# The reciprocal root of x moved from the query projection into the key projection, in a layer whose order is fixed by a planner

## The chip, the cores and the metric

The kernel runs on one core of a Trainium2 chip. The metric is the time of one execution on the device in microseconds (us). The core's engines are TensorE (PE; its weight loads are shown apart as PEld), VectorE (DVE), ScalarE (ACT), GpSimd (POOL) and SyncE (SP, which here issues the large transfers). Each engine works off its own instructions in order, and they wait for one another through semaphores.

## The reference, cut to what matters

```python
# x: (1, 256, 2048); 16 meta tokens are put ahead, so h has 272 rows
u = rms_norm(h, norm_mix)                 # h * rsqrt(mean(h*h) + 1e-6) * gain
proj = einsum('bld,dc->blc', u, w_in)     # 2048 -> aq, ak, av (1024 each), mq, mk, mv, mo, mg
aq, ak, av, mq, mk, mv, mo, mg = split(proj)
attn_out = diff_attention(rope(aq), rope(ak), av, ...)   # 8 heads, two softmaxes each
ml_out = mlstm_mixer(mq, mk, mv, mo, mg, ...)            # mg: the gates, 16 columns
h = h + concat(attn_out, ml_out) @ w_out
u = rms_norm(h, norm_ffn)
h = h + (silu(u @ w_gate) * (u @ w_up)) @ w_down         # 2048 -> 5632 -> 2048
return rms_norm(h, norm_final)[:, 16:]
```

The factor `rsqrt(mean(h*h))` is one number for each token. The kernel does not scale x by it ahead of the projections: it multiplies the unscaled x by the weights (with the gain put into the weights), and puts the factor in behind them. For queries and keys it goes into the rotary tables (`ropeC`, `ropeS`), which multiply them anyway; for the gates it is a multiplication by `rbc`, a tile that holds the factor of each token on every partition.

## The kernel before, in words

Every product is made in three parts for accuracy. A weight w is split into a high part `wh` and the rest `wl` (lines 205 and 206: ACT makes `wh` with the gain `gm`, DVE makes `wl` from `raw`, `gm` and `wh`), the activation into `uh` and `ul`, and PE adds `wh`·`uh`, `wh`·`ul` and `wl`·`uh` (lines 251, 252 and 253). Weights come in pieces of 256 rows by 512 columns (512 KB, loaded by SP into `raw_...`), each split in two halves of 128x512. There are four buffers of each of `raw`, `wh` and `wl`. A projection of 512 columns has 8 pieces and four accumulators; per piece there are 24 matmuls.

The stages follow one another on PE: the first half of the query projection (`aq_0` to `aq_7`, line 426, together with the transposes of x and their splits `uhl`, lines 405 and 406), then of the key projection (`ak`) and of the value projection (`av`), then the second halves of the three, the projections of the second mixer, the output projection, and the feed-forward part.

The order on each engine is made by a planner: it simulates the program with costs of its own and puts an instruction where it expects it to be ready. `pin(instruction)` keeps an instruction in program order. In a projection a `slot()` is called at every second piece; it takes the next step of the generators in the list `urgent`, so that small work comes between the matmuls of the large one.

The parts that the change touches:

- `x_rstd` (lines 344 to 355) makes the reciprocal root of the three token groups in 14 small steps on DVE and writes it out wide as `rmat` (line 355). It is run, pinned, among the last weight splits of the query projection (`rstd_steps`). `x_broadcast` (lines 357 to 365) turns it into a row on every partition with three matmuls into `prs` (a small PSUM tile, of which there are two) and copies that to `rbc` on ACT (line 365). Then DVE and POOL multiply the rotary tables by it (lines 489 and 490).
- `setup` transposes small vectors and makes the factor lambda (`lexp`, `nlam`, line 509).
- `gates` makes the gates of the second mixer: POOL multiplies the gate weights `wg` by the gain (line 564), ACT casts them to `wgp` (line 565), PE makes `pgate`, DVE multiplies it by `rbc` to `gsb` (line 574), PE makes `psi` (line 585), and a chain of small steps follows: `gi_ga` and `gfr` on DVE (lines 586 to 589), abs, exp and log on ACT (590 to 592), then on DVE `gi_ga` (594), two running sums (596, 597), a subtraction (600), two running maxima (603, 604) and more. The end of it, `pct`, is a set of transposes on PE.
- `rope` rotates a head pair: a shuffle and a multiplication on DVE (lines 840 and 841), a multiplication and an addition on POOL (842 and 843). `value_copy` takes an accumulator out of PSUM into `vt_...` on ACT (line 631).
- `in_proj(..., pins=n)` pins the splits of the first n pieces; before, the first key projection has 4 and the value projection none.

Of the kernel before, what the change touches and what calls it, by code (L numbers as in the profile page):

```python
# [86 lines left out]
def tile_hybrid_encoder_layer(  # L87
# [36 lines left out]
    def sm_tile(name):  # L124
        return smp.tile([P, N_CHUNK], F32, tag="sm", name=name)
# [4 lines left out]
    def f(ap):  # L130
        return ap.bitcast(F32)
# [66 lines left out]
    def pin(ins):  # L198
        tc.keep_in_program_order(ins)
# [86 lines left out]
    rmat = ep.tile([P, 3, P], F32, name="rmat")  # L286
# [48 lines left out]
    def x_square(i):  # L335
# [4 lines left out]
                accum_out=ssx[:, 4 * b + c:4 * b + c + 1],  # L340
            )
        )

    def x_rstd():
        ms, y, t, h = (rs3[:, 3 * i:3 * i + 3] for i in range(4))
        yield V.tensor_reduce(ms[:, 0:2], ssx[:, :8].rearrange("p (b c) -> p b c", c=4), AX.X, ALU.add)
        yield V.tensor_copy(ms[:, 2:3], ssx[:, 8:9])
        yield V.tensor_scalar(ms, ms, 1.0 / D, EPS, ALU.mult, ALU.add)
        yield V.tensor_scalar(y.bitcast(I32), ms.bitcast(I32), -0.5, RSQRT_MAGIC, ALU.mult, ALU.add)
        yield V.tensor_scalar(h, ms, -0.5, None, ALU.mult)  # L350
        for _ in range(3):
            yield V.tensor_tensor(t, y, y, ALU.mult)
            yield V.tensor_tensor(t, t, h, ALU.mult)
            yield V.scalar_tensor_tensor(y, t, 1.5, y, ALU.add, ALU.mult)
        yield V.tensor_copy(rmat, rs3[:, 3:6, None].to_broadcast([P, 3, P]))

    def x_broadcast():
        prs = sm_tile("prs")
        pin(T.matmul(prs[:, :NM], lhsT=rmat[:NM, 2, :], rhs=ident[:NM, :NM], start=True, stop=True))
        for b in range(NB):  # L360
            pin(T.matmul(
                prs[:, NM + b * P:NM + (b + 1) * P], lhsT=rmat[:, b, :], rhs=ident,
                start=True, stop=True,
            ))
# [67 lines left out]
    rstd = x_rstd()

    def rstd_steps(n):
        for _ in range(n):
            ins = next(rstd, None)
            if ins is not None:
                pin(ins)
# [121 lines left out]
    colt = mp.tile([P, 5, 64], F32, name="colt")  # L560

    def gates():
        wgp = mp.tile([P, KD, 32], F32R, tag="t2", bufs=3, name="wgp")
        G.tensor_tensor(wg, wg, gm[:, :, None].to_broadcast([P, KD, 16]), ALU.mult)
        A.copy(wgp[:, :, :16], wg)
# [267 lines left out]
    def rope(ps, t0, name, h):  # L833
        n = NT - t0
        if t0:
            qk[h] = pair_tile(f"qk{h}")
        dst = qk[h][:, 0 if t0 else 1, :n]
        sh = mp.tile([P, NT], F32, tag="ev", bufs=4, name=f"sh_{name}")
        swap = list(range(8, 16)) + list(range(8)) + list(range(16, 32))
        V.stream_shuffle(sh[:, :n], ps[:, :n], swap)  # L840
        V.tensor_tensor(dst, ps[:, :n], ropeC[:, t0:], ALU.mult)
        G.tensor_tensor(sh[:, :n], sh[:, :n], ropeS[:, t0:], ALU.mult)
        G.tensor_tensor(dst, dst, sh[:, :n], ALU.add)
        return dst
# [7 lines left out]
    def attention(h0, nh):  # L852
        es, at, hs, on, qs, ks = {}, {}, {}, {}, {}, {}

        def stack(h):
            q, k = aq[h], ak[h]
            qs[h] = mp.tile([P, 2, SEQ], F32R, tag="qs", bufs=2, name=f"qs{h}")
            ks[h] = mp.tile([P, 2, 2, HT], F32R, tag="ks", bufs=2, name=f"ks{h}")
            kz = klow[h % 2]
            for c in range(2):  # L860
                own, other = slice(64 * c, 64 * c + 64), slice(64 - 64 * c, 128 - 64 * c)
                A.activation(qs[h][own, c, :], q[own], AF.Copy, scale=QK_SCALE)
                kc = apart(k[own])
                A.copy(ks[h][own, c], kc)
                A.copy(ks[h][other, c], kc)
                V.scalar_tensor_tensor(
                    qs[h][other, c, :], q[own], QK_SCALE, f(qs[h][own, c, :]), ALU.mult, ALU.subtract
                )
                V.tensor_tensor(kz[own, c], kc, f(ks[h][own, c]), ALU.subtract)

        def stats(h):
            g = h // 2
# [81 lines left out]
                yield  # L954
        attending.remove(h0)

    def roping(vts, t0, dst, name, g):
        def hook(i):
            if 1 <= i <= 4:
                dst[4 * g + i - 1] = rope(vts[i - 1], t0, f"{name}_{4 * g + i - 1}", 4 * g + i - 1)  # L960

        return hook

    for g in range(2):
        if g:
# [15 lines left out]
        urgent.append(value_natural(vts, lambda j, g=g: val[:, :, 4 * g + j, :], f"a{g}"))  # L981
        pending.append(attention(4 * g, 4))
# [256 lines left out]
```

## Time and profile before

| | us |
|---|---|
| median of 3 runs | 1125.45 |
| the three runs | 1124.95, 1125.45, 1127.51 |
| profiled execution | 1124.79 |
| its span | 1123.0 |
| query projection, PE, first to last matmul | 5.9 to 36.6 |
| key projection begins, value projection begins | 36.6, 64.1 |
| next query projection begins | 90.4 |

The span is the time from the first to the last instruction in the profile. A row of the timeline has the start, the duration, the engine, the line, the operation, what it writes and reads, and in square brackets how long the engine was idle before it and what it waited for.

### The profile page before, as it was taken

How to read it: one execution, taken by the hardware profiler on the slowest of the kernel's cores; microseconds unless marked ns; L12 is line 12 of the kernel's file. 1: busy time of each engine (PE TensorE's matmuls, PEld its weight loads, DVE VectorE, ACT ScalarE, POOL GpSimd, SP SyncE). 2: the span in 40 equal slices, each digit the busy share in tenths (PEclk: the TensorE clock that was granted, in tenths of full speed). 3: DMA queues.
4: the chain of work that ended last, by engine and by line, in shares of the span. 5: the costliest groups of instructions: out<-in, count | busy, mean ns of one | idle time of the engine just before them, and what ended most of it. 6: DMA issues, size and time to landing. Idle time of an engine off the chain costs nothing.

```text
span 1123.0 us, 18984 instructions
## 1 busy us (share of the span) xinstructions
PE 1108.5 (99%) x7181; PEld 1025.4 (91%) x7181; DVE 737.6 (66%) x1151; ACT 659.3 (59%) x1205; POOL 243.9 (22%) x315
## 2 busy tenths in 40 slices
PE   9999999999999999999999999999999999999997
PEld 8999999999999989999999999999999888888896
DVE  6996987988785987655655655655655645454544
ACT  6578888788976555554554554554554544344443
POOL 7330240010043944122122122122122100000000
PEclk9999999999999999999999999999999999999998
DMA  9556555555445675575665665665665766666663
GB/s 276 169 149 205 147 165 159 152 151 154 148 152 160 202 235 179 192 228 184 199 220 184 200 217 188 201 213 187 205 209 187 251 205 198 205 192 204 193 204 111
DMA packets 112539, 212.78 MB, mean 189 GB/s; under 512 B 8938, under 2 KB 10288, under 8 KB 112304
## 3 DMA queue, kind: packets, MB, share of 16 engines
q1 hardware_dynamic: 111664, 209.95, 59.8%
q10 hardware_dynamic: 464, 1.58, 0.4%
q8 instruction: 56, 0.92, 0.3%
q14 instruction: 35, 0.29, 0.1%
q0 software_dynamic: 320, 0.04, 0.0%
HBM read 209.45 MB, written 2.10 MB: 188 GB/s over the span
## 4 chain that ended last, share of the span: by engine, by line
PE 92%; DVE 4%; DMA 1%; issue 1%; ACT 1%; SPq 1%; POOL 0%; DVEq 0%; ACTq 0%; POOLq 0%
PE acc_up L248 14%; PE acc_ga L248 14%; PE acc_ga L249 7%; PE acc_up L249 7%; PE acc_dn L1129 7%; PE acc_dn L1126 7%; PE acc_dn L1130 7%; PE acc_wo L248 3%; PE acc_mo L248 3%; PE acc_wo L249 2%; PE acc_mv L251 1%; PE acc_mv L253 1%; PE acc_mv L252 1%; PE acc_mo L249 1%; PE acc_av L253 1%; PE acc_av L251 1%
## 5 line engine op out<-in xcount | busy, mean ns | idle before, releaser
L248 PE MATMUL acc_ga<-vhl,wh_ga 128*128 128x512 f32 x704 | 226.0, 382 | 0.0
L248 PE MATMUL acc_up<-vhl,wh_up 128*128 128x512 f32 x704 | 225.5, 382 | 0.0
L213 DVE TENSOR_TENSOR wl_dn<-raw_dn,wh_dn 128x1024 fp32r<-128x1024 f32 x88 | 108.5, 1234 | 116.2 <-ACT wh_dn L212 116.1
L249 PE MATMUL acc_ga<-vhl,wl_ga 128*128 128x256 f32 x704 | 176.7, 273 | 0.0
L249 PE MATMUL acc_up<-vhl,wl_up 128*128 128x256 f32 x704 | 175.8, 273 | 0.0
L213 DVE TENSOR_TENSOR wl_up<-raw_up,wh_up 128x1024 fp32r<-128x1024 f32 x88 | 114.6, 1342 | 81.2 <-ACT wh_up L212 81.1
L212 ACT CAST wh_dn<-raw_dn 128x1024 fp32r<-128x1024 f32 x88 | 92.4, 1051 | 126.0 <-PE acc_dn L1130 114.3
L213 DVE TENSOR_TENSOR wl_ga<-raw_ga,wh_ga 128x1024 fp32r<-128x1024 f32 x88 | 104.3, 1225 | 67.5 <-ACT wh_ga L212 67.5
L248 PEld LDWEIGHTS acc_ga<-vhl,wh_ga 128*128 128x128 f32 x704 | 130.2, 190 | 15.0
L248 PEld LDWEIGHTS acc_up<-vhl,wh_up 128*128 128x128 f32 x704 | 129.9, 190 | 14.7
L1126 PE MATMUL acc_dn<-wh_dn,ffh 128*128 128x512 f32 (+1 forms) x396 | 141.2, 357 | 0.0
L1130 PE MATMUL acc_dn<-wh_dn,ffl 128*128 128x512 f32 (+1 forms) x396 | 141.2, 357 | 0.0
L1129 PE MATMUL acc_dn<-wl_dn,ffh 128*128 128x512 f32 (+1 forms) x396 | 140.9, 356 | 0.0
L249 PEld LDWEIGHTS acc_up<-vhl,wl_up 128*128 128x128 f32 x704 | 134.7, 191 | 3.8
L249 PEld LDWEIGHTS acc_ga<-vhl,wl_ga 128*128 128x128 f32 x704 | 134.8, 191 | 3.7
L212 ACT CAST wh_ga<-raw_ga 128x1024 fp32r<-128x1024 f32 x88 | 89.0, 1048 | 67.4 <-PE acc_ga L248 32.9
L212 ACT CAST wh_up<-raw_up 128x1024 fp32r<-128x1024 f32 x88 | 89.0, 1048 | 55.2 <-PE acc_up L248 20.1
L1130 PEld LDWEIGHTS acc_dn<-wh_dn,ffl 128*128 128x128 f32 x396 | 75.1, 190 | 8.2
L1129 PEld LDWEIGHTS acc_dn<-wl_dn,ffh 128*128 128x128 f32 x396 | 75.1, 190 | 8.1
L1126 PEld LDWEIGHTS acc_dn<-wh_dn,ffh 128*128 128x128 f32 x396 | 75.0, 190 | 8.0
L248 PE MATMUL acc_wo<-mix,wh_wo 128*128 128x512 f32 x224 | 73.3, 382 | 0.0
L1087 POOL TENSOR_TENSOR s<-s,rbf 128x256 f32<-128x256 f32 x44 | 33.1, 754 | 173.3 <-DVE s L269 173.2
(365 smaller groups left out, 2441.2 us busy)
## 6 DMA issues: line engine op xcount, KB each, us to landing
raw_ga<-in_w_gate_dram SPq DMA_DIRECT2D x88, 512.0 KB, 4.6
raw_up<-in_w_up_dram SPq DMA_DIRECT2D x88, 512.0 KB, 4.6
raw_dn<-in_w_down_dram SPq DMA_DIRECT2D x88, 512.0 KB, 4.8
raw_wo<-in_w_out_dram SPq DMA_DIRECT2D x32, 512.0 KB, 4.4
raw_ak<-in_w_in_dram SPq DMA_DIRECT2D x16, 512.0 KB, 4.2
raw_av<-in_w_in_dram SPq DMA_DIRECT2D x16, 512.0 KB, 4.1
raw_mv<-in_w_in_dram SPq DMA_DIRECT2D x16, 512.0 KB, 3.9
raw_mo<-in_w_in_dram SPq DMA_DIRECT2D x16, 512.0 KB, 4.0
```

What stands on the lines that cost most here:

```text
L212: pin(A.copy(wh, raw))
L213: pin(V.tensor_tensor(wl, raw, f(wh), ALU.subtract))
L248: T.matmul(pair, lhsT=qh[:, kk, sl], rhs=both(k), start=first, stop=False)
L249: T.matmul(pair[:, 1], lhsT=ql[:, kk, sl], rhs=xh(k), start=False, stop=last)
L251: T.matmul(o, lhsT=qh[:, kk, sl], rhs=xh(k), start=first, stop=False)
L252: T.matmul(o, lhsT=qh[:, kk, sl], rhs=xl(k), start=False, stop=False)
L253: T.matmul(o, lhsT=ql[:, kk, sl], rhs=xh(k), start=False, stop=last)
L1087: G.tensor_tensor(s1, s1, rbf, ALU.mult)
L1126: mm = T.matmul(o, lhsT=ffh[:, k, bsl], rhs=ph, start=(k == 0), stop=False)
L1129: T.matmul(o, lhsT=ffh[:, k, bsl], rhs=pl, start=False, stop=False)
L1130: T.matmul(o, lhsT=ffl[:, k, bsl], rhs=ph, start=False, stop=(k == KF - 1))
```

## The change

`x_rstd` and `x_broadcast` become one generator `x_rms`, put into `urgent` ahead of `setup` and `gates`. Only its first step, the reduction, is pinned, behind the query projection's work; the rest is left to the planner. `rmat` is now written by ACT and lies in another pool, the rotary tables' multiplications are no longer pinned, and `gates` has an empty step more at its start. The rotation of the first queries is called from within the key projection (pieces 4 to 7) and not ahead of it. The splits of all 8 pieces of the first value projection are pinned, and so are the splits of queries and keys of the first head.

```diff
-    def x_rstd():
-        ms, y, t, h = (rs3[:, 3 * i:3 * i + 3] for i in range(4))
-        yield V.tensor_reduce(ms[:, 0:2], ssx[:, :8].rearrange("p (b c) -> p b c", c=4), AX.X, ALU.add)
...
-        yield V.tensor_copy(rmat, rs3[:, 3:6, None].to_broadcast([P, 3, P]))
-
-    def x_broadcast():
-        prs = sm_tile("prs")
-        pin(T.matmul(prs[:, :NM], lhsT=rmat[:NM, 2, :], rhs=ident[:NM, :NM], start=True, stop=True))
...
-        pin(A.copy(rbc, prs[:, :NT]))
...
-        if k >= 10:
-            rstd_steps(4 if k < 13 else 16)
...
-        if j == 1:
-            x_broadcast()
...
-    pin(V.tensor_tensor(ropeC, ropeC, rbc, ALU.mult))
-    G.tensor_tensor(ropeS, ropeS, rbc, ALU.mult)
+
+    def x_rms():
+        ms, y, t, h = (rs3[:, 3 * i:3 * i + 3] for i in range(4))
+        rmat = mp.tile([P, 3, P], F32, tag="t2", bufs=3, name="rmat")
+        pin(V.tensor_reduce(ms[:, 0:2], ssx[:, :8].rearrange("p (b c) -> p b c", c=4), AX.X, ALU.add))
+        V.tensor_copy(ms[:, 2:3], ssx[:, 8:9])
+        V.tensor_scalar(ms, ms, 1.0 / D, EPS, ALU.mult, ALU.add)
+        rsqrt(ms, y, t, h)
+        A.copy(rmat, y[:, :, None].to_broadcast([P, 3, P]))
+        yield
+        prs = sm_tile("prs")
+        T.matmul(prs[:, :NM], lhsT=rmat[:NM, 2, :], rhs=ident[:NM, :NM], start=True, stop=True)
...
+        A.copy(rbc, prs[:, :NT])
+        V.tensor_tensor(ropeC, ropeC, rbc, ALU.mult)
+        G.tensor_tensor(ropeS, ropeS, rbc, ALU.mult)
+        yield
...
     def gates():
+        yield
         wgp = mp.tile([P, KD, 32], F32R, tag="t2", bufs=3, name="wgp")
...
+            order = unpinned if h else pin
...
+                order(A.activation(qs[h][own, c, :], q[own], AF.Copy, scale=QK_SCALE))
...
         if g == 0:
-            for i in range(1, 5):
-                hook(i)
-            hook = None
+            urgent.append(x_rms())
             urgent.append(setup())
             urgent.append(gates())
...
-        accs = in_proj(C_AV + g * N_CHUNK, 0, f"av{g}", hook=roping(vts, 0, ak, "ak", g))
+        accs = in_proj(
+            C_AV + g * N_CHUNK, 0, f"av{g}", pins=0 if g else 8, hook=roping(vts, 0, ak, "ak", g)
+        )
```

The orders differ from the start of the last third of the query projection to some 130 us of the span, and are the same behind that; the sequence of SP's transfers is the same throughout. Lines of the changed kernel stand 15 to 24 lower in number: its `wh` and `wl` are still 205 and 206, `value_copy` is 615, the rope's two DVE steps are 824 and 825, the gate's chain is 570 to 588.

ACT at the end of the query projection, where `wh_aq_6` is the high part of the seventh piece, `uhl` a split of x. Before:

```order
L405 CAST uhl<-ptx_386 128x2x128
L205 ACTIVATE wh_aq_6_393<-raw_aq_6_391,gm 128x512
L565 CAST wgp<-wg 128x16x16
L405 CAST uhl<-ptx_415 128x2x128
L205 ACTIVATE wh_aq_6_393<-raw_aq_6_391,gm 128x512
```

The same place in the changed order, and then ACT from the first key piece on:

```order
L381 CAST uhl<-ptx_385 128x2x128
L205 ACTIVATE wh_aq_6_392<-raw_aq_6_390,gm 128x512
L381 CAST uhl<-ptx_410 128x2x128
L205 ACTIVATE wh_aq_6_392<-raw_aq_6_390,gm 128x512
```

```order
L461 COPY rmat<-rs_96 128x384
L205 ACTIVATE wh_ak_1_607<-raw_ak_1_605,gm 128x512 x2
L549 CAST wgp<-wg 128x16x16
L205 ACTIVATE wh_ak_2_650<-raw_ak_2_648,gm 128x512 x2
L205 ACTIVATE wh_ak_3_682<-raw_ak_3_680,gm 128x512 x2
L205 ACTIVATE wh_ak_4_762<-raw_ak_4_760,gm 128x512 x2
L470 COPY rbc<-prs 128x272
```

The cast of the gate weights has moved from between the query splits to behind the second key piece, and the copy of `prs` stands behind the splits of four more key pieces.

DVE from the key to the value projection, where `gi_ga`, `gfr` and `gF_gx` are the gate chain, `wl_av_0` the low part of the first value piece, `sh_ak` and `qk` the rope of the keys. Before:

```order
L589 TENSOR_SCALAR gfr<-gfr 64x272
L206 SCALAR_TENSOR_TENSOR wl_av_0_948<-raw_av_0_945,gm,wh_av_0_947 128x512 x2
L594 SCALAR_TENSOR_TENSOR gi_ga<-gfr,gi_ga 64x272
L596 SCALAR_TENSOR_TENSOR gF_gx<-ones,gi_ga 32x272
L597 SCALAR_TENSOR_TENSOR gF_gx<-ones,gi_ga 32x256
L206 SCALAR_TENSOR_TENSOR wl_av_1_985<-raw_av_1_982,gm,wh_av_1_984 128x512
L600 TENSOR_TENSOR gi_ga<-gi_ga,gF_gx 64x272
```

Changed:

```order
L578 SCALAR_TENSOR_TENSOR gi_ga<-gfr,gi_ga 64x272
L824 STREAM_SHUFFLE sh_ak_1051<-vt_k_924 128x272
L580 SCALAR_TENSOR_TENSOR gF_gx<-ones,gi_ga 32x272
L581 SCALAR_TENSOR_TENSOR gF_gx<-ones,gi_ga 32x256
L825 TENSOR_TENSOR qk_830<-vt_k_924,cst 128x272
L584 TENSOR_TENSOR gi_ga<-gi_ga,gF_gx 64x272
L824 STREAM_SHUFFLE sh_ak_1088<-vt_k_926 128x272
L825 TENSOR_TENSOR qk_858<-vt_k_926,cst 128x272
L587 SCALAR_TENSOR_TENSOR gF_gx<-ones,gi_ga 32x272
L588 SCALAR_TENSOR_TENSOR gF_gx<-ones,gi_ga 32x256
L206 SCALAR_TENSOR_TENSOR wl_av_0_940<-raw_av_0_937,gm,wh_av_0_939 128x512 x2
```

The splits of the first value piece stood ahead of the gate's sums and now stand behind its sums and its maxima and behind the rope of two key tiles.

PE at the same boundary. Before:

```order
L252 MATMUL acc_ak_3_605<-uhl,wh_ak_7_871 128x272
L253 MATMUL acc_ak_3_605<-uhl,wl_ak_7_872 128x272
L251 MATMUL acc_av_0_933<-uhl,wh_av_0_947 128x272
L252 MATMUL acc_av_0_933<-uhl,wh_av_0_947 128x272
L253 MATMUL acc_av_0_933<-uhl,wl_av_0_948 128x272
```

Changed:

```order
L253 MATMUL acc_ak_3_558<-uhl,wl_ak_7_867 128x272
L599 MATMUL pct<-ident,gi_ga 16x64
L601 MATMUL pct<-ident,gi_ga 128x64
L251 MATMUL acc_av_0_928<-uhl,wh_av_0_939 128x272
L252 MATMUL acc_av_0_928<-uhl,wh_av_0_939 128x272
L251 MATMUL acc_av_1_929<-uhl,wh_av_0_939 128x272
L252 MATMUL acc_av_1_929<-uhl,wh_av_0_939 128x272
L251 MATMUL acc_av_2_930<-uhl,wh_av_0_939 128x272
L252 MATMUL acc_av_2_930<-uhl,wh_av_0_939 128x272
L251 MATMUL acc_av_3_931<-uhl,wh_av_0_939 128x272
L252 MATMUL acc_av_3_931<-uhl,wh_av_0_939 128x272
L253 MATMUL acc_av_0_928<-uhl,wl_av_0_940 128x272
```

The gate's transposes `pct` stand between the last key matmul and the first value matmul, and the first value matmul that reads a low part comes after eight that read the high one. `psi` stood ahead of 96 key matmuls before and stands ahead of 48 now.

More of the change, by code (lines that the diff above doesn't have):

```diff
@@ L285, in tile_hybrid_encoder_layer @@
     scr = ep.tile([P, D], F32, name="scr")
-    rmat = ep.tile([P, 3, P], F32, name="rmat")
     cols = persist.tile([P, P], F32, name="cols")
@@ L342, in x_square @@
         )
-    def x_rstd():
-        ms, y, t, h = (rs3[:, 3 * i:3 * i + 3] for i in range(4))
-        yield V.tensor_reduce(ms[:, 0:2], ssx[:, :8].rearrange("p (b c) -> p b c", c=4), AX.X, ALU.add)
[L347 to L355, printed above, removed]
-    def x_broadcast():
-        prs = sm_tile("prs")
[L359 to L364, printed above, removed]
-        pin(A.copy(rbc, prs[:, :NT]))
     def meta_columns():
@@ L430, in aq_matmul @@
         )
[L432 to L438, printed above, removed]
     def prepare(k):
@@ L488, in tile_hybrid_encoder_layer @@
     ropeS = cst[:, K_S:K_S + NT]
-    pin(V.tensor_tensor(ropeC, ropeC, rbc, ALU.mult))
-    G.tensor_tensor(ropeS, ropeS, rbc, ALU.mult)
+    def x_rms():
[9 more added lines that the diff above has]
+        T.matmul(prs[:, :NM], lhsT=rmat[:NM, 2, :], rhs=ident[:NM, :NM], start=True, stop=True)
+        for b in range(NB):
+            T.matmul(
+                prs[:, NM + b * P:NM + (b + 1) * P], lhsT=rmat[:, b, :], rhs=ident,
+                start=True, stop=True,
+            )
[3 more added lines that the diff above has]
+        yield
     nlam = mp.tile([P, 1], F32, name="nlam")
@@ L859, in stack @@
             kz = klow[h % 2]
+            order = unpinned if h else pin
             for c in range(2):
                 own, other = slice(64 * c, 64 * c + 64), slice(64 - 64 * c, 128 - 64 * c)
-                A.activation(qs[h][own, c, :], q[own], AF.Copy, scale=QK_SCALE)
                 kc = apart(k[own])
-                A.copy(ks[h][own, c], kc)
-                A.copy(ks[h][other, c], kc)
-                V.scalar_tensor_tensor(
+                order(A.activation(qs[h][own, c, :], q[own], AF.Copy, scale=QK_SCALE))
+                order(A.copy(ks[h][own, c], kc))
+                order(A.copy(ks[h][other, c], kc))
+                order(V.scalar_tensor_tensor(
                     qs[h][other, c, :], q[own], QK_SCALE, f(qs[h][own, c, :]), ALU.mult, ALU.subtract
-                )
-                V.tensor_tensor(kz[own, c], kc, f(ks[h][own, c]), ALU.subtract)
+                ))
+                order(V.tensor_tensor(kz[own, c], kc, f(ks[h][own, c]), ALU.subtract))
         def stats(h):
@@ L955, in attention, with roping @@
         attending.remove(h0)
-    def roping(vts, t0, dst, name, g):
+    def roping(vts, t0, dst, name, g, i0=1):
         def hook(i):
-            if 1 <= i <= 4:
-                dst[4 * g + i - 1] = rope(vts[i - 1], t0, f"{name}_{4 * g + i - 1}", 4 * g + i - 1)
+            if i0 <= i < i0 + 4:
+                dst[4 * g + i - i0] = rope(vts[i - i0], t0, f"{name}_{4 * g + i - i0}", 4 * g + i - i0)
         return hook
@@ L967, in tile_hybrid_encoder_layer @@
         vts = value_copy(accs, f"q{g}", SEQ, split=g > 0)
-        hook = roping(vts, NM, aq, "aq", g)
+        hook = roping(vts, NM, aq, "aq", g, 1 if g else 4)
         if g == 0:
-            for i in range(1, 5):
-                hook(i)
-            hook = None
+            urgent.append(x_rms())
             urgent.append(setup())
@@ L978, in tile_hybrid_encoder_layer @@
         vts = value_copy(accs, f"k{g}")
-        accs = in_proj(C_AV + g * N_CHUNK, 0, f"av{g}", hook=roping(vts, 0, ak, "ak", g))
+        accs = in_proj(
+            C_AV + g * N_CHUNK, 0, f"av{g}", pins=0 if g else 8, hook=roping(vts, 0, ak, "ak", g)
+        )
         vts = value_copy(accs, f"a{g}")
```

## The prediction

> **What bounds the kernel now.** I read the page first, then the windows, then TensorE's own waits, and last the timelines of the two places that the change touches. The page's head and its engines:
>
> ```profile
> span 1123.0 us, 18984 instructions
> PE 1108.5 (99%) x7181; PEld 1025.4 (91%) x7181; DVE 737.6 (66%) x1151; ACT 659.3 (59%) x1205; POOL 243.9 (22%) x315
> ```
>
> TensorE (PE) is busy for 1108.5 of 1123.0 us, so the change can only move what is left, and only where PE waits. The windows tell where that is (columns: length, then the busy time of PE, PEld, DVE, ACT and POOL, the granted clock, the DMA share, GB/s):
>
> ```profile
> 30.00:40.00 10.00, 9.11 (x71) 8.32 (x71) 9.23 (x30) 7.11 (x15) 3.41 (x4) 1.00 0.56 159
> 60.00:70.00 10.00, 8.80 (x76) 8.60 (x76) 9.87 (x21) 7.04 (x15) 4.21 (x4) 1.00 0.31 97
> 400.00:1110.00 710.00, 710.00 (x4125) 645.88 (x4124) 405.38 (x443) 352.80 (x485) 120.74 (x155) 1.00 0.63 200
> 1110.00:1123.00 13.00, 4.82 (x44) 4.63 (x42) 5.92 (x23) 4.50 (x10) 0.00 (x0) 0.77 0.44 161
> ```
>
> From 400 to 1110 PE has no gap at all. At 30 to 40 (the end of the query projection) and at 60 to 70 (from the key to the value projection) it loses 0.9 and 1.2 us, and there VectorE (DVE) is busy for 9.23 and 9.87 of 10: in these two places DVE's order sets PE's waits. What PE waited for (us in total, times, longest):
>
> ```profile
> PE acc_av L253 <- DVE wl_av L206: 1.8, 2, 1.2
> ...
> PE acc_aq L426 <- DVE uhl L406: 0.5, 1, 0.5
> PE pat L901 <- DVE e L894: 0.4, 1, 0.4
> PE acc_aq L426 <- DVE wl_aq L206: 0.3, 1, 0.3
> ```
>
> All of them are waits for DVE, and none is over 1.2 us.
>
> **The change part by part.** The sum is made against the profiled execution, 1124.79 us (span 1123.0); the median, 1125.45, lies 0.66 above it, which I add at the end.
>
> A, the end of the query projection, where the steps of the reciprocal root leave DVE and the gate weights' cast (wgp) leaves ScalarE (ACT):
>
> ```profile
> 27.59 0.41 ACT L565 CAST wgp<-wg 128x256 fp32r<-128x256 f32 x1 [1.30 <-POOL wg L564]
> 30.30 0.17 DVE L353 TENSOR_TENSOR rs<-rs 128x3 f32<-128x3 f32 x1
> 33.62 0.55 DVE L355 COPY rmat<-rs 128x384 f32<-128x384 f32 x1
> 29.69 0.39 PE L426 MATMUL acc_aq<-uhl,wh_aq 128*128 128x256 f32 x2
> 33.59 0.39 PE L426 MATMUL acc_aq<-uhl,wh_aq 128*128 128x256 f32 x2
> 33.92 0.39 PE L426 MATMUL acc_aq<-uhl,wh_aq 128*128 128x256 f32 x2
> 34.14 0.28 PE L426 MATMUL acc_aq<-uhl,wl_aq 128*128 128x256 f32 x1
> ```
>
> Three matmuls in step take 33.92 - 33.59 = 0.33, so 0.11 each. The 24 that start from 29.69 to 34.14 would need 23 x 0.112 = 2.6 and took 4.45: 1.9 are lost. In that time DVE runs ten small steps at 0.17 and the copy of 0.55, 2.2 us in all, between the splits for which PE waits, and the splits on ACT start 1.30 late because of the cast. With both gone the end of the loss is at best 1.9 and, if the splits themselves still lag by half a microsecond, 1.3. I take -1.7.
>
> The broadcast's matmuls (prs) move from here into the key projection:
>
> ```profile
> 34.35 0.39 PE L359 MATMUL prs<-ident,rmat 16*128 16x16 f32 x2
> 35.14 0.47 PE L426 MATMUL acc_aq<-uhl,wh_aq 128*128 128x256 f32 x2
> 30.54 2.55 ACT L205 ACTIVATE wh_ak<-raw_ak,gm 128x512 fp32r<-128x512 f32 x4
> 61.75 0.75 DVE L206 SCALAR_TENSOR_TENSOR wl_av<-raw_av,gm,wh_av 128x512 fp32r<-128x512 f32 x1
> ```
>
> They cost 35.14 - 34.35 = 0.79 here and the same there: 0. B, what is new is their wait. The 14 dependent steps of the root, at 0.17 to 0.2 each (2.6), then rmat's copy on ACT, stand ahead of them behind the first key weights' splits, and there PE has the first piece of the key projection (24 matmuls, 2.8) to cover that. So 0 to 0.9; I take +0.5. C, the broadcast's copy out of PSUM (L470) stands on ACT behind the key weights' splits of four pieces, at 2.55 / 4 = 0.64 each; prs holds one of two small PSUM buffers until then, and the next to need one, the gate projection, may wait. 0 if the splits run ahead of PE, one split, 0.6, if not: +0.3. Both queues behind these waits (PE's own, ACT's splits) are in the figures. SP's DMAs are issued in the same sequence: 0. POOL's steps keep theirs but for the gate weights' product, one slot later; nothing waits for it before the gate projection, whose wait is C's: 0.
>
> D, the gate chain. In the changed order the transposes of the gate (pct, L599 and L601) stand on PE ahead of every matmul of the value projection. Before, they come later, and what is between psi and the gate's result hides behind value matmuls. The chain's rows as they ran before:
>
> ```profile
> 52.24 0.72 PE L585 MATMUL psi<-gsb,cst 32*128 32x273 f32 x2 [0.27 <-DVE gsb L574]
> 52.90 0.38 PE L251 MATMUL acc_ak<-uhl,wh_ak 128*128 128x272 f32 x1
> 54.90 0.48 DVE L587 TENSOR_SCALAR gi_ga<-psi,bi 64x272 f32<-64x272 f32 x1
> 56.35 0.35 DVE L589 TENSOR_SCALAR gfr<-gfr 64x272 f32<-64x272 f32 x1
> 57.10 0.41 ACT L590 ACTIVATE gi_ga<-gfr 64x272 f32<-64x272 f32 x1
> 58.00 1.28 ACT L592 ACT_TABLE_LOAD   x1
> 59.85 0.43 DVE L594 SCALAR_TENSOR_TENSOR gi_ga<-gfr,gi_ga 64x272 f32<-64x272 f32 x1 [1.81 <-ACT gi_ga L592]
> 61.04 0.68 DVE L597 TENSOR_TENSOR_SCAN gF_gx<-ones,gi_ga 32x256 f32<-32x256 f32 x1
> 62.42 0.42 DVE L600 TENSOR_TENSOR gi_ga<-gi_ga,gF_gx 64x272 f32<-64x272 f32 x1
> 63.45 0.46 DVE L840 STREAM_SHUFFLE sh_ak<-vt_k 128x272 f32<-128x272 f32 x1
> 63.80 0.41 DVE L841 TENSOR_TENSOR qk<-vt_k,cst 128x272 f32<-128x272 f32 x1
> 64.14 1.28 DVE L603 TENSOR_TENSOR_SCAN gF_gx<-ones,gi_ga 32x272 f32<-32x272 f32 x1
> 65.43 1.10 DVE L604 TENSOR_TENSOR_SCAN gF_gx<-ones,gi_ga 32x256 f32<-32x256 f32 x1
> 63.98 0.86 POOL L842 TENSOR_TENSOR sh_ak<-sh_ak,cst 128x272 f32<-128x272 f32 x1 [16.21 <-DVE sh_ak L840]
> 64.92 1.06 POOL L843 TENSOR_TENSOR qk<-qk,sh_ak 128x272 f32<-128x272 f32 x1
> ```
>
> From the end of psi: on DVE bi and gi_ga to gfr, 56.35 + 0.35 - 54.90 = 1.8, with bi (0.1) and one rope multiply (0.4) that now stands between: 2.3. On ACT from 57.10 to 59.85, 2.75, with one copy of a key accumulator between, of about the size of the 0.41 step: 3.1. On DVE gi_ga and the two sums, 61.04 + 0.68 - 59.85 = 1.9, a shuffle and a multiply (0.35 each by their spacing) and the subtraction, 0.4: 3.0. Together 8.4. The cover: in the changed order 48 key matmuls stand behind psi.
>
> ```profile
> 64.00 0.28 PE L253 MATMUL acc_ak<-uhl,wl_ak 128*128 128x272 f32 x1
> 64.12 0.28 PE L251 MATMUL acc_av<-uhl,wh_av 128*128 128x272 f32 x1
> 68.41 0.28 PE L252 MATMUL acc_av<-uhl,wh_av 128*128 128x272 f32 x1
> 69.88 0.38 PE L253 MATMUL acc_av<-uhl,wl_av 128*128 128x272 f32 x1 [1.20 <-DVE wl_av L206]
> ```
>
> At 64.12 - 64.00 = 0.116 they give 5.6 us. So PE waits 8.4 - 5.6 = 2.8 if nothing slows the chain. But the key rope's work runs on POOL meanwhile, and the two later scans took 1.28 and 1.10 beside POOL's two rope steps, where the sum at 61.04 took 0.68: 1.75 times as long. If all of the last 3.0 is slowed so, 2.2 is added, 5.0 in all. The sums start before most of the rope's steps reach POOL, so I stay near the lower end: +3.4.
>
> The Trainium skill (SBUF — State Buffer, Who interferes with whom) says that a DVE instruction with two SBUF inputs contends with a GpSimd one that reads SBUF, and that the one issued first has the shared ports while the other fully blocks. The trace agrees (1.28 against 0.68); by this rule alone every step of D under a rope step would wait it out, and the sum would go to D's upper end, 1.6 higher.
>
> E, the next wait. The low parts of the first value weights (wl_av_0) now stand on DVE behind a shuffle, a multiply and two more scans, that is behind 0.7 and 1.4 to 2.4 us of work after the gate's result, and take 0.7: 2.8 to 3.8. From the same moment PE has the two transposes (about 0.25) and eight matmuls on the high part, 0.93, then needs wl_av_0. The wait is 1.6 to 2.6, and 0.5 more if its own split is slowed by 1.75 too. The rope steps are on POOL by now, so I take +2.6.
>
> F, what goes. The two waits for wl_av (1.8; the first costs 69.88 - 68.41 - 0.116 = 1.36, so 0.16 more than the wait) and psi's 0.3: 2.1 to 2.6. These splits are now ahead of PE, since D and E hold PE up. I take -2.5.
>
> G, past the value projection the two orders join by about 130 us, at steps like pat (0.4). I take 0, between -1.0 and +1.0: one such wait gone or doubled, at two or three places.
>
> Sum: -1.7 + 0.5 + 0.3 + 3.4 + 2.6 - 2.5 = +2.6. 1124.79 + 2.6 = 1127.4; against the median, 1128.0.
>
> **The rivals.** A measurement of this kernel tells about 0.2%, 2.25 us, from no change.
>
> 1. No measurable change. D and E run without POOL in the way: 2.8 + 1.6 in place of 6.0, and C is 0: 1.9 less, 1126.1. For it: the sums at 61.04 took 0.68. Against it: the scans of E fall where the rope's steps fall.
>
> 2. Faster. The gate's chain ends inside its cover: then D is 0, and with it the queue that pushes E. The point is 5.6 us: psi to the gate's result would have to take 2.8 us less than its rows say, for instance if psi ran one group of 24 matmuls (2.8) further ahead. Then A, F and half of E remain, -1.7 + 0.8 - 2.5 + 1.3 = -2.1: 1123.3. Against it: the table load of 1.28 and the two ACT steps can't be hidden, and psi itself waits for gsb.
>
> 3. Slower by more: the clock. PE has no wait over 1.4 us before; now there are two, 3.4 and 2.6, about 1 us apart. In the window from 1110, where PE is busy for only 4.82 of 13 us, the granted clock is 0.77; at 60 to 70, with 1.2 us lost, it is 1.00. If the clock halves for the first 3.5 us after the waits, 1.8 is lost: 1129.8.
> The Trainium skill (TensorE: Matmul & The Clock Gate, What's actually happening) puts the clock at half after one idle window of about 3.4 us that runs freely; D would then be on the edge of it, and no row of the trace before has a wait of that length amid matmuls.
>
> **How the numbers follow.** The forecast, two waits of 3.4 and 2.6 at the start of the value projection, 1126.8 to 1129.4 by their ends: 0.60. Rival 1: 0.22. Rival 2: 0.06. Rival 3: 0.12. The predicted time is the forecast's, 1128.0. The range goes down to 1125.5, below rival 1's 1126.1, and up past rival 3 with D at 5.0 and G at 0: 1130.8; it leaves out rival 2 and the tails. Faster by over 0.2% (under 1123.2) is half of rival 2 and a part of rival 1's lower tail, 0.05. Slower by over 0.2% (above 1127.7) is rival 3 and three quarters of the forecast, 0.57. The rest, 0.38, is within 0.2%.
>
> **What would show it.** A: PE's waits for uhl and wl_aq are gone from its list and the query projection ends 1.5 us or so earlier, net of the 0.8 that moved. B and C: prs and the gate projection wait under a microsecond each. D: pct waits 2.8 to 5.0 for DVE's subtraction, right after the last key matmul. E: eight value matmuls later, wl_av waits 1.6 to 3.2. F: no further wait for wl_av. From 400 us on nothing differs. The prediction is wrong if pct finds its gate ready, if psi's place on PE turns out to be earlier in time than its rows in the order suggest, or if a wait over 1 us shows up past the value projection.

## The result: the profile after, and where the time went

| | before | changed |
|---|---|---|
| median, us | 1125.45 | 1130.31 (5 runs, 1128.62 to 1132.05) |
| ratio to before, 95% interval | | 1.004 [1.0028, 1.0052] |
| profiled execution, span | 1124.79, 1123.0 | 1128.62, 1126.8 |

The changed kernel is slower, by 3.8 us in the profiled executions and 4.9 in the medians; the forecast was 1128.0 in a range of 1125.5 to 1130.8. At the end of the first three pairs of projections its profiled execution is 4.8 us behind (the first matmul after them starts at 175.67 and not 170.90); what follows takes one of two times, 951.1 or 952.2 us, in whichever kernel, and here the changed kernel happened to have the shorter one. Its head, its engines and the windows that answer to those of before (columns: length, busy time of PE, PEld, DVE, ACT and POOL, granted clock, DMA share, GB/s):

```profile
span 1126.8 us, 18992 instructions
PE 1108.4 (98%) x7181; PEld 1026.7 (91%) x7181; DVE 732.9 (65%) x1150; ACT 658.5 (58%) x1206; POOL 246.5 (22%) x315
```

```profile
30.00:40.00 10.00, 10.00 (x85) 9.69 (x84) 7.00 (x31) 6.78 (x15) 1.06 (x1) 1.00 0.49 156
60.00:70.00 10.00, 4.87 (x34) 4.30 (x32) 8.35 (x17) 5.59 (x11) 7.42 (x8) 0.84 0.01 2
70.00:80.00 10.00, 9.80 (x68) 9.60 (x69) 7.95 (x16) 7.03 (x11) 0.00 (x0) 0.82 0.61 162
400.00:1110.00 710.00, 710.00 (x4127) 646.30 (x4127) 407.61 (x446) 353.61 (x486) 123.94 (x157) 1.00 0.63 201
```

The gap at 30 to 40 us is closed. At 60 to 70 PE is busy for 4.87 of 10 us where it was 8.80, and the granted clock, 1.00 everywhere there before, is 0.84 and 0.82 over twenty microseconds. What PE waited for (total, times, longest):

```profile
PE pct L599 <- DVE gi_ga L584: 3.5, 1, 3.5
PE acc_av L253 <- DVE wl_av L206: 1.8, 1, 1.8
...
PE acc_ak L251 <- DVE hs L877: 1.2, 1, 1.2
PE pgate L555 <- ACT lexp L490: 0.3, 1, 0.3
```

The lines left out are waits in the first 17 us (for the DMA of x and for POOL), which both kernels have. The waits for uhl, wl_aq and psi are gone. The wait for hs is new and stands in the second key projection:

```profile
125.88 0.35 PE L251 MATMUL acc_ak<-uhl,wh_ak 128*128 128x272 f32 x1 [1.16 <-DVE hs L877]
```

PE at the start of the value projection:

```profile
62.47 0.28 PE L253 MATMUL acc_ak<-uhl,wl_ak 128*128 128x272 f32 x1
66.28 0.21 PE L599 MATMUL pct<-ident,gi_ga 64*16 64x64 f32 x1 [3.54 <-DVE gi_ga L584]
...
66.49 0.38 PE L251 MATMUL acc_av<-uhl,wh_av 128*128 128x272 f32 x1
...
67.97 0.43 PE L252 MATMUL acc_av<-uhl,wh_av 128*128 128x272 f32 x1
70.20 0.59 PE L253 MATMUL acc_av<-uhl,wl_av 128*128 128x272 f32 x1 [1.80 <-DVE wl_av L206]
...
73.82 0.28 PE L251 MATMUL acc_av<-uhl,wh_av 128*128 128x272 f32 x1
```

From the last key matmul to pct 3.81 us pass where one step is 0.116: 3.7 lost. The eight matmuls after pct take (67.97 - 66.49) / 7 = 0.21 each, near twice the step, and then PE waits for wl_av_0; from 66.49 to 70.20 it does what is 0.93 us of work at full clock: 2.8 lost. The low clock has no part in these 2.8, since DVE makes wl_av_0 no earlier; at full clock the wait would have been longer by as much. The next 16 matmuls take 73.82 - 70.20 = 3.62 and not 1.86, so here the low clock costs 1.8, if the splits for the matmuls behind would have been ready that much earlier, which no run shows. The windows of that stretch:

```profile
62.00:66.00 4.00, 0.75 (x7) 0.54 (x5) 3.37 (x7) 3.61 (x8) 2.76 (x4) 1.00 0.00 0
66.00:70.00 4.00, 2.12 (x10) 1.76 (x10) 3.95 (x7) 0.00 (x0) 2.74 (x3) 0.60 0.00 0
70.00:74.00 4.00, 3.80 (x18) 3.80 (x19) 3.00 (x7) 2.27 (x4) 0.00 (x0) 0.55 0.47 131
74.00:78.00 4.00, 4.00 (x35) 3.80 (x35) 2.95 (x6) 4.00 (x7) 0.00 (x0) 1.00 0.66 156
```

DVE in that time:

```profile
62.58 0.43 DVE L578 SCALAR_TENSOR_TENSOR gi_ga<-gfr,gi_ga 64x272 f32<-64x272 f32 x1 [1.28 <-ACT gi_ga L576]
...
63.31 0.91 DVE L580 TENSOR_TENSOR_SCAN gF_gx<-ones,gi_ga 32x272 f32<-32x272 f32 x1
64.23 1.09 DVE L581 TENSOR_TENSOR_SCAN gF_gx<-ones,gi_ga 32x256 f32<-32x256 f32 x1
...
66.98 1.28 DVE L587 TENSOR_TENSOR_SCAN gF_gx<-ones,gi_ga 32x272 f32<-32x272 f32 x1
68.28 1.09 DVE L588 TENSOR_TENSOR_SCAN gF_gx<-ones,gi_ga 32x256 f32<-32x256 f32 x1
69.40 2.08 DVE L206 SCALAR_TENSOR_TENSOR wl_av<-raw_av,gm,wh_av 128x512 fp32r<-128x512 f32 x3
```

It begins the gate's sums just as the key projection ends, and wl_av_0 is behind sums and maxima.

A table by stage helps with the experiments: PE's time from one stage's first matmul to the next one's, in the profiled executions. The query projection is counted from the transposes of the meta tokens (at 16 to 19 us) on, since what lies ahead of them differs by up to 3.3 us between the executions. What follows the first three pairs of projections took 951.1 to 952.3 us in all of them. The first column is the least certain: in eleven executions, of kernels whose DVE and ACT do the same steps in the same order up to there as in the changed kernel, it was 17.2 to 18.7 us, and 18.00 in the changed kernel's own second profile. The other columns of that second profile agree with the first within 0.1.

| kernel | end of query | key | value | second query | second key |
|---|---|---|---|---|---|
| before | 20.16 | 27.53 | 26.33 | 25.24 | 28.06 |
| changed | 17.23 | 32.68 | 27.89 | 24.33 | 29.81 |
| no pins on the value splits | 18.68 | 28.78 | 25.35 | 24.33 | 29.81 |
| no pins, no empty step | 17.95 | 28.24 | 24.44 | 24.34 | 29.74 |
| the root's move alone | 17.74 | 28.25 | 29.34 | 25.24 | 28.10 |
| before with the empty step | 19.21 | 28.28 | 27.94 | 25.24 | 28.06 |

### The profile page after: what moved, and what is told of

It is laid out like the page before. It is cut to its first block, busy times and chain, and to the rows that moved or that the text cites. A ratio compares the mean times of both kernels' runs of the same rounds, so it can differ in the third digit from the quotient of the medians.

```text
span 1126.8 us, 18992 instructions
## 1 busy us (share of the span) xinstructions
PE 1108.4 (98%) x7181; PEld 1026.7 (91%) x7181; DVE 732.9 (65%) x1150; ACT 658.5 (58%) x1206; POOL 246.5 (22%) x315
## 4 chain that ended last, share of the span: by engine, by line
PE 95%; DVE 2%; ACT 1%; DMA 1%; issue 0%; SPq 0%; DVEq 0%; ACTq 0%
PE acc_up L248 14%; PE acc_ga L248 14%; PE acc_ga L249 7%; PE acc_up L249 7%; PE acc_dn L1111 7%; PE acc_dn L1115 7%; PE acc_dn L1114 7%; PE acc_wo L248 4%; PE acc_mo L248 3%; PE acc_wo L249 2%; PE acc_aq L402 2%; PE acc_av L253 1%; PE acc_mv L251 1%; PE acc_av L251 1%; PE acc_mv L253 1%; PE acc_mv L252 1%
```

## The experiments

**The pins on the value splits.** Each edit here is against the changed kernel unless it says otherwise, and each ratio is to the kernel before, measured again beside it (medians 1124.92 to 1125.93).

```diff
-            C_AV + g * N_CHUNK, 0, f"av{g}", pins=0 if g else 8, hook=roping(vts, 0, ak, "ak", g)
+            C_AV + g * N_CHUNK, 0, f"av{g}", hook=roping(vts, 0, ak, "ak", g)
```

> The changed kernel with the splits of the first value projection no longer pinned; the planner then puts wl_av_0 right behind wl_ak_7 on DVE, ahead of the gate chain, and the gate's transposes 144 matmuls later on PE. Theory (the loss stands at the start of the value projection, in DVE's queue, and the clock falls after it): the waits for pct (3.5) and wl_av (1.8) and the stretch at half clock go, the gain of 2 us in the query projection stays: 1121 to 1123.5 us, granted clock 1.00 at 60 to 80. Rival (the loss comes from the broadcast in the key projection or from later stages): 1128 or more.

Measured: 1123.87 us, ratio 0.9992 [0.9984, 1.0001]. Both long waits are gone, and the largest left there is 0.64; the key and the value projection together take 54.1 us against 60.6 in the changed kernel. So the loss stands where the forecast put it, and the pins on the value splits make it. The time, 0.4 above the expected stretch, isn't told from before.

**Only the transposes moved back.**

```diff
+        yield
+        yield
         pct = sm_tile("pct")
```

> The changed kernel with two empty steps ahead of the gate's transposes: on PE these move 230 matmuls back, behind most of the value projection, and DVE's order stays as it was. Theory (DVE's queue, with the two running maxima ahead of wl_av_0, sets the start): PE runs eight value matmuls and then waits for wl_av_0 once, for 5 to 7 us, until about the same moment as before (70 us); the time stays at 1129 to 1132 us. Rival (the transposes' place on PE is the cause): their wait of 3.5 us goes and the time falls to 1126 to 1127.

Measured: 1128.89, ratio 1.004 [1.0026, 1.0053], 0.1 below the expected stretch. PE, in time:

```profile
63.78 0.38 PE L251 MATMUL acc_av<-uhl,wh_av 128*128 128x272 f32 x1 [1.10 <-ACT wh_av L205]
...
70.13 0.60 PE L253 MATMUL acc_av<-uhl,wl_av 128*128 128x272 f32 x1 [5.15 <-DVE wl_av L206]
```

With pct out of the way PE reaches wl_av_0 earlier and waits for it until 70.13, where it was 70.20. The place of the transposes on PE costs little by itself (the key and the value projection together take 59.8 us and not 60.6): DVE's queue sets when the value projection starts. And even wh_av_0, on ACT behind the copies of all four key accumulators, comes 1.1 late.

**Which pin.** In the changed order wh_av_0 stands behind those copies, the last of which needs the last key matmul. Two runs pin only the first piece, and only the others.

```diff
-            C_AV + g * N_CHUNK, 0, f"av{g}", pins=0 if g else 8, hook=roping(vts, 0, ak, "ak", g)
+            C_AV + g * N_CHUNK, 0, f"av{g}", pins=0 if g else 1, hook=roping(vts, 0, ak, "ak", g)
```

> The changed kernel with only the first piece of the first value projection pinned (1 in place of 8). In its order wh_av_0 still stands on ACT behind the copies of all four key accumulators, and the gate's transposes, sums and maxima ahead of wl_av_0. Theory (the pin of that one piece makes the whole loss): waits for pct of 3.5 and for wl_av of about 1.8 and half clock behind them as in the changed kernel, 1128.5 to 1131 us. Rival (the pins of the seven later pieces have a part, by holding later splits back): 1 us or more below the changed kernel, 1126 to 1128.

Measured: 1130.04, ratio 1.0042 [1.0029, 1.0054], with waits of 3.54 for pct and 1.59 for wl_av. The pin of the first piece is enough for the whole loss.

```diff
-                wh, wl = load_piece(src, kp * CK, c0, f"{name}_{kp}", gain, pin if i < pins else unpinned)
+                wh, wl = load_piece(src, kp * CK, c0, f"{name}_{kp}", gain, pin if (i < pins and (i > 0 or pins == 4)) else unpinned)
```

> The changed kernel with the second to the eighth piece pinned and the first free: wh_av_0 and wl_av_0 stand ahead of the gate chain again, the gate's transposes 48 matmuls later. Theory: neither wait nor half clock at 62 to 74 us, a few waits under 1 us later, 1122.5 to 1125 us, the same as with no pins within 1 us. Rival (the later pins cost on their own): over 1126.

Measured: 1129.58, ratio 1.0034 [1.0021, 1.0047]: the theory was wrong here. The value projection starts in time, and the loss is back 48 matmuls later:

```profile
69.85 0.22 PE L599 MATMUL pct<-ident,gi_ga 64*16 64x64 f32 x1 [0.61 <-DVE gi_ga L584]
69.91 0.22 PE L601 MATMUL pct<-ident,gi_ga 64*128 64x64 f32 x1
74.25 0.36 PE L602 MATMUL pct<-ident,gnm 64*128 64x64 f32 x1 [4.11 <-ACT gnm L595]
```

With wh_av_2 pinned behind the end of the gate chain on ACT, the planner puts all of pct ahead of the third piece, and PE waits 4.11 for its last input. The transposes aren't the cause here either: ACT itself comes to wh_av_2 only then.

```profile
74.10 5.00 ACT L205 ACTIVATE wh_av<-raw_av,gm 128x512 fp32r<-128x512 f32 x8
```

So it isn't one pin: both that were tried put a value split behind the gate chain and open a gap on PE, and the planner puts into the gap transposes that themselves wait for the chain.

**The clock.** The first of two runs fills the gap with matmuls on constants.

```diff
+        accs = [acc_tile(f"acc_av{g}_{j}") for j in range(4)]
+        if g == 0:
+            for i in range(28):
+                pin(T.matmul(
+                    accs[0][:, :P], lhsT=vts[3][:, :P] if i == 0 else ones[:, :P], rhs=ones[:, :P],
+                    start=True, stop=True,
+                ))
...
-            C_AV + g * N_CHUNK, 0, f"av{g}", pins=0 if g else 8, hook=roping(vts, 0, ak, "ak", g)
+            C_AV + g * N_CHUNK, 0, f"av{g}", pins=0 if g else 8, hook=roping(vts, 0, ak, "ak", g), accs=accs
```

> The changed kernel with 28 matmuls on constants, results unused, put on PE ahead of the first value matmul, the first of them behind the copy of the last key accumulator; DVE's order is the same. They add about 6.5 us of PE work into a stretch in which PE waits. Theory (the two waits bring the clock to half, and that costs 1.8 us in the profiled run and makes the runs differ by 3 us): the clock stays at 1.00, matmuls behind the wait for wl_av_0 start 0.116 apart and not 0.228, and the time falls by 0.5 to 2.5 us to 1128 to 1130 with a spread under 1 us. Rival (the clock is no cost of its own): 1131 or more, since the first value matmuls now stand behind the added ones.

Measured: 1134.38, ratio 1.0081 [1.0067, 1.0094], runs from 1132.81 to 1135.93. On the clock the expectation held up to 99 us, on the time it did not; the time is in the rival's stretch. Each added matmul shows as two records:

```profile
66.13 6.19 PE L965 MATMUL acc_av<-ones 128*128 128x128 f32 x54
...
72.78 0.38 PE L253 MATMUL acc_av<-uhl,wl_av 128*128 128x272 f32 x1 [0.22 <-DVE wl_av L206]
...
73.66 0.28 PE L251 MATMUL acc_av<-uhl,wh_av 128*128 128x272 f32 x1
73.78 0.28 PE L252 MATMUL acc_av<-uhl,wh_av 128*128 128x272 f32 x1
...
99.14 0.38 PE L647 MATMUL pv_a<-ident,vt_a 128*16 128x128 f32 x1 [2.74 <-ACT vt_a L615]
```

Steps of 0.12 directly behind the stretch, clock 1.00. But the order of later steps changed too, with a new wait of 2.74 that ends at 99.14, behind which the clock falls after all (0.50 at 100 to 102 us), and this execution reached the meta transposes 2.6 later than the changed kernel's. The run shows that a busy PE keeps its clock at the start of the value projection; it doesn't price the fall in the time. That the runs are no closer together (3.1 us) doesn't tell much, since the kernel before, whose clock stays at 1.00 at this place, spread by 4.0 us in the 23 runs beside this one.

The second shortens the chain, so that no wait should be as long as 3.4 us.

```diff
-        V.tensor_tensor_scan(gF[:32], ones[:32], ga[:32], 0.0, ALU.mult, ALU.add)
+        V.tensor_tensor_scan(gF[:32, :32], ones[:32, :32], ga[:32, :32], 0.0, ALU.mult, ALU.add)
         V.tensor_tensor_scan(
-            gF[32:64, NM:][:, ::-1], ones[32:64, NM:], ga[32:64, NM:][:, ::-1], 0.0, ALU.mult, ALU.add
+            gF[32:64, SEQ - 16:][:, ::-1], ones[32:64, SEQ - 16:], ga[32:64, SEQ - 16:][:, ::-1], 0.0, ALU.mult, ALU.add
```

> The changed kernel with the two running sums of the gate chain cut to 32 columns, which leaves most of them out. The chain ahead of pct is 1.5 to 1.8 us shorter. Theory for the wait (D is the chain's length less its cover): pct waits 1.8 to 2.1 and not 3.5, and wl_av some 2 as before. For the clock, theory 1 (it falls on idle time summed over some microseconds, as 1.7 and 0.4 did in the run with the empty step alone): half clock again behind the waits, 1127.5 to 1129.5. Theory 2 (it needs one wait of about 3.4): the clock stays at 1.00 at 60 to 80 and the time is 1125.5 to 1127.5.

Measured: 1129.32, ratio 1.0032 [1.002, 1.0044]. The wait for pct fell to 2.66 (0.9 less, not 1.5 or more, since the short sums still took 0.41 and 0.71, where the full ones took 0.91 and 1.09), the one for wl_av was 2.12, and the clock fell all the same:

```profile
66.15 0.21 PE L599 MATMUL pct<-ident,gi_ga 64*16 64x64 f32 x1 [2.66 <-DVE gi_ga L584]
69.67 0.59 PE L253 MATMUL acc_av<-uhl,wl_av 128*128 128x272 f32 x1 [2.12 <-DVE wl_av L206]
```

```profile
66.00:70.00 4.00, 1.73 (x11) 1.49 (x12) 3.96 (x6) 0.37 (x1) 3.09 (x3) 0.78 0.00 0
70.00:72.00 2.00, 2.00 (x10) 2.00 (x10) 2.00 (x5) 1.58 (x2) 0.23 (x1) 0.50 0.00 0
```

No single wait of 3.4 us is needed.

**The empty step alone, in the kernel before.**

```diff
     def gates():
+        yield
         wgp = mp.tile([P, KD, 32], F32R, tag="t2", bufs=3, name="wgp")
```

> The kernel before with one edit of the change alone: the empty step at the start of gates. The gate weights' cast leaves ACT's query splits and psi moves back; the reciprocal root stays in the query projection. Theory (two causes share the 2.1 us lost at the end of the query projection, the cast's 1.3 us on ACT and the root's steps on DVE): 0.8 to 1.5 us faster there, nothing lost later since wl_av_0 to wl_av_1 stand ahead of the gate chain on DVE: 1123 to 1124.8. Rival (the cast alone cost it all): 1122.5 to 1123.3; rival (the root's steps alone): 1125 to 1126.

Measured: 1126.26, ratio 1.0009 [1.0001, 1.0018]. The edit doesn't do what was expected of the cast: it stands where it stood, between the query splits, with the same idle time ahead of it.

```profile
27.91 0.41 ACT L566 CAST wgp<-wg 128x256 fp32r<-128x256 f32 x1 [1.30 <-POOL wg L565]
```

So this run can't part the cast from the root's steps, and what each of them costs stays open. That the end of the query projection is 0.95 shorter all the same (20.16 to 19.21), as forecast, is luck: up to its last split ACT, and DVE to its end, do the same steps in the same order as in the kernel before, and in this execution PE reached the meta transposes 1.27 later (17.70) and the key projection 0.32 later (36.91). What the edit did move is psi, which has 48 key matmuls behind it and not 96. That nothing is lost later was wrong:

```profile
78.24 0.38 PE L253 MATMUL acc_av<-uhl,wl_av 128*128 128x272 f32 x1 [1.53 <-DVE wl_av L206]
79.09 0.38 PE L253 MATMUL acc_av<-uhl,wl_av 128*128 128x272 f32 x1 [0.24 <-DVE wl_av L206]
```

```profile
78.00:80.00 2.00, 1.52 (x9) 1.32 (x9) 2.00 (x6) 1.59 (x3) 0.00 (x0) 0.88 0.00 0
80.00:82.00 2.00, 2.00 (x10) 2.00 (x10) 2.00 (x5) 1.97 (x4) 0.00 (x0) 0.50 0.89 249
```

A later gate chain meets the split of the keys (`klow`): on DVE two steps of it (73.11 to 75.04), the gate's two maxima and `klow` once more stand ahead of wl_av (77.43), and the clock fell to half behind waits of 1.53 and 0.24.

**The first head's splits.** Two runs free them as well; the second is, of the whole change, only the root's move and the rotation inside the key projection.

```diff
-            order = unpinned if h else pin
+            order = unpinned
...
-            C_AV + g * N_CHUNK, 0, f"av{g}", pins=0 if g else 8, hook=roping(vts, 0, ak, "ak", g)
+            C_AV + g * N_CHUNK, 0, f"av{g}", hook=roping(vts, 0, ak, "ak", g)
```

> The changed kernel with neither the value splits nor the splits of the first head's queries and keys pinned. Theory (the wait of 1.16 us in the second key projection, which all kernels with that pin have, comes from the attention's first steps being held back): that wait goes and the two stages from 89 to 143 us take 53.3 as before and not 54.1; 1122 to 1124 us, 0 to 1 below the kernel with no pins on the value splits alone. Rival (the wait comes from the order elsewhere): 54.1 stays, no difference.

Measured: 1126.76, ratio 1.0009 [1.0, 1.0018], over the expected stretch. The wait for hs goes and the second query and key projections take 53.3 us, as expected; but the value projection takes 28.45 and not 25.35, and the sum is worse than with the pin:

```profile
78.44 0.38 PE L253 MATMUL acc_av<-uhl,wl_av 128*128 128x272 f32 x1 [1.89 <-DVE wl_av L206]
```

```profile
76.00:80.00 4.00, 1.87 (x14) 1.47 (x14) 3.90 (x8) 1.39 (x3) 0.00 (x0) 1.00 0.13 49
80.00:84.00 4.00, 4.00 (x37) 4.00 (x36) 3.90 (x7) 3.72 (x6) 0.00 (x0) 1.00 0.85 228
```

Here a wait of 1.89, with one of 0.24 at 79.30, left the clock at 1.00.

**The version that is left.** Value splits free, and no empty step:

```diff
     def gates():
-        yield
         wgp = mp.tile([P, KD, 32], F32R, tag="t2", bufs=3, name="wgp")
...
-            C_AV + g * N_CHUNK, 0, f"av{g}", pins=0 if g else 8, hook=roping(vts, 0, ak, "ak", g)
+            C_AV + g * N_CHUNK, 0, f"av{g}", hook=roping(vts, 0, ak, "ak", g)
```

> The changed kernel with the value splits not pinned and without the empty step in gates; the gate weights' cast still stands behind the query splits on ACT, and psi comes 48 key matmuls earlier. Theory (the gain in the query projection comes from the root's steps and the cast leaving, not from the empty step; nothing in the value projection waits for the gate chain): query projection 2 us shorter as in the changed kernel, waits for wl_av under 1 us each, clock 1.00 throughout: 0.5 to 2 us below before. Rival (the earlier gate chain is in DVE's way in the key projection): the key projection longer by 1 us or more, no gain over before.

Measured: 1122.12, ratio 0.9975 [0.9965, 0.9984]: 2.8 us below before, more than the 0.5 to 2 expected, and faster than both kernels by more than the 0.2%, though against before that bound lies inside the interval. The key projection is 0.7 longer than before, about the 0.8 of prs, which moved there, so the rival is out. The windows and the largest wait of the value projection:

```profile
60.00:70.00 10.00, 9.51 (x80) 9.11 (x79) 9.90 (x21) 5.66 (x11) 6.78 (x6) 1.00 0.24 75
70.00:80.00 10.00, 10.00 (x88) 9.80 (x88) 9.86 (x17) 6.67 (x12) 4.35 (x3) 1.00 0.71 190
```

```profile
68.95 0.38 PE L253 MATMUL acc_av<-uhl,wl_av 128*128 128x272 f32 x1 [0.45 <-DVE wl_av L206]
```

The same with the first head's splits free too (`order = unpinned`, the first edit under "The first head's splits"):

> As the last one, with the splits of the first head's queries and keys not pinned either: of the change only the root's move, its broadcast in the key projection and the rotation of the queries inside it are left. Theory (the free splits of the head bring klow back onto DVE in the value projection, ahead of wl_av, and cost there what the pinned ones cost in the second key projection and more): one or two waits for wl_av of 1 to 2 us in the value projection, no wait for hs; 0 to 2 us above the kernel with those splits pinned. Rival (the pins of the head have no part): within 0.5 us of it.

Measured: 1124.78, ratio 1.0003 [0.9994, 1.0013], 2.7 us above the version with the pin.

```profile
70.05 0.38 PE L253 MATMUL acc_av<-uhl,wl_av 128*128 128x272 f32 x1 [2.38 <-DVE wl_av L206]
71.47 0.59 PE L253 MATMUL acc_av<-uhl,wl_av 128*128 128x272 f32 x1 [0.81 <-DVE wl_av L206]
```

Its clock is 0.83 at 70 to 80, and the value projection takes 29.34 against 24.44. So the root's move by itself gains about 1.7 in the query and the key projection of these executions (2.42 less and 0.72 more than before) and gives it back in the value projection. With the root moved, the pin of the head's splits, which the prediction left out, is what keeps the gain; the pin without the root's move wasn't run. `klow` is not what delays wl_av here, as the theory had it: it comes behind it on DVE (71.34). Ahead of that wl_av stand the gate's maxima on DVE, and ahead of its wh_av (67.30) four casts of the first head's keys on ACT.

The changed kernel once more, on the chip of these two:

> The changed kernel once more, beside the other two on one chip. Theory: pct waits 3.5, wl_av 1.6 to 2, half clock for 5 to 8 us behind them, ratio to before 1.003 to 1.005. Rival (the loss of the first measurement was that chip's): a ratio within 1.002.

Measured: 1130.88, ratio 1.0052 [1.0038, 1.0065], with waits of 3.54 for pct and 1.74 for wl_av. The loss isn't one chip's.

## Why the prediction was right, and what it missed

The way and the places were right: two waits at the start of the value projection, for pct and then for wl_av, slower by over 0.2%. The size was about half: +2.6 forecast, +4.8 up to the end of the three pairs of projections, +4.9 between the medians. The measured time lies 0.5 below the upper end of the range and nearer to rival 3 than to the forecast. By its steps:

- A, -1.7: 20.16 - 17.23 - 0.79 (prs, which moved) = -2.1 in these two executions, and between -0.7 and -2.1 by the executions with the changed order. What of it is the cast's and what the root's steps', no run shows.
- B and C, +0.8: the key projection grew by 5.15, of which prs is 0.8, pct 0.2 and D 3.7; about 0.45 is left. prs waits for nothing, so B is 0; C is the wait of 0.33 for pgate, released by `lexp`, which ACT does (42.04) right behind the copy of prs (41.77). The psi wait (0.27) is gone inside that.
- D, +3.4: 3.54 waited, 3.7 lost, and by the way forecast: from psi's end (56.99) to the gate's result (66.14) 9.15 us, where the forecast had 8.4 and 0.6, less the cover of 5.6. The sums were slowed beside POOL's rope steps, to 0.91 and 1.09.
- E, +2.6: 2.8 lost. Only 1.80 of it shows as a wait, because the eight matmuls ahead ran at half clock; wl_av_0 was ready no earlier, as with pct moved back, where PE got it at 70.13.
- F, -2.5: both early waits for wl_av and the one for psi are gone. The value projection grew by 1.56, so beside E's 2.8 and the clock's 1.8 some 3.0 went.
- G, 0: the second query and key projections took 0.84 longer, with a wait of 1.16 for hs. The time lies within the bounds given, but a wait over 1 us past the value projection was one of the prediction's own signs of being wrong, and it came. The two runs without the pin of the first head's splits don't have it, so it comes with that pin, which the prediction didn't price.
- The bounds don't add up as written. D from 2.8 to 5.0 and E from 1.6 to 3.1 put the forecast between 1126.4 and 1130.1, not 1126.8 and 1129.4; rival 3 with D at 5.0 is 1131.4, and 1130.8 is rival 3 with G at +1.0.
- The clock is the step that failed. It stood as a rival of its own at 1129.8 and a chance of 0.12, priced at 1.8; 1.8 is what the steps behind the second wait show. But it was no alternative to the forecast: where D and E come true, PE is idle for 5.3 of 7.7 us (62.47 to 70.20), and in all the runs with these two waits the clock fell with them. It belonged into the sum, which would have been +4.4. The reason I gave against it, that 1.2 us of loss had left the clock at 1.00, was one sample of something that goes either way.

The Trainium skill (TensorE: Matmul & The Clock Gate, What's actually happening) has the clock at half after an idle window of about 3.4 us that runs freely. The changed kernel agrees: 0.60 and 0.55 behind a wait of 3.54. The run with the short sums (2.66 and 2.12) and the one with the empty step (1.53 and 0.24) fell with no idle stretch of that length, so its number isn't a limit below which a wait is safe.

The rule on the shared ports (the Trainium skill, SBUF — State Buffer, Who interferes with whom), by which D would have gone to its upper end, did not change the result. The trace agrees with it in part: the second sum took 1.09, as much as a slowed row of before (1.10), the first 0.91, between the free 0.71 and the slowed 1.28, and the subtraction (0.43), with no rope step beside it, wasn't slowed, so D stayed near its lower end.

What stays open: how much of the time the low clock costs, since no run has the changed order at full clock, and what the cast and the root's steps each cost in A. That the changed kernel's runs lie 1128.62 to 1132.05 apart is nothing of its own: the kernel before spread by 4.0 us in 23 runs. Part of that shows in the traces of every kernel (the meta transposes were reached between 15.9 and 19.2 us, and the time behind the three pairs of projections is one of about 951.1 and 952.2).

## What to carry to other kernels

A pin for good order in one queue decides in all queues: the planner fills the gap that it makes on TensorE with whatever it thinks ready, here transposes at the end of a long chain, and each engine then waits in order. Where a forecast has TensorE wait for 2.4 us or more at a time, as in the eight executions named below, the fall of the clock is a term of the sum and no separate case: about 1.8 us here, for the matmuls behind the last wait; what runs slowly ahead of a wait costs nothing more. Move one thing at a time: here the root's move gains nothing without the pin of the first head's splits, and the pins of the value splits, put in with them, hid that. And look in the trace whether an edit did what it was meant to do, before a number that fits is taken for its effect.

## What the runs showed of the hardware

The granted clock fell to 0.50 behind waits of 1.53 and 0.24 us in one kernel (the kernel before with the empty step) and stayed at 1.00 behind 1.89 and 0.24 in another (value splits and the first head's splits free) and behind 1.20 and 0.56 in the kernel before. So neither the length of such waits settles it nor their sum: 1.77 fell, 1.76 and 2.13 did not. In the eight executions with a longer wait (2.38, 2.66, 2.74, three times 3.54, 4.11 and 5.15 us) it fell each time.

How long it stayed at half comes in two lengths: 3.4 us in three executions (79.5 to 82.9 in the kernel before with the empty step) and 6.8 us in the other six (66.8 to 73.6 in the changed kernel), as the granted clock in windows of half a microsecond shows.

A scan (running sum or maximum) of 32x272 took DVE 0.71 us with POOL idle, as the first sum of the kernel before, and 1.28 beside POOL's rope steps, as its first maximum; 32x256 took 0.68 and 1.10.
